# Loads in the order of first use at the start and between the two FFN stages, and a longer allowance for weight loads, in a Macaron transformer block

## The chip, the core and the metric

The kernel runs on one core of a Trainium2 chip. The core has TensorE (PE, matrix products), VectorE (DVE), ScalarE (ACT) and GpSimd (POOL), which run side by side and wait for each other by semaphores. SyncE (SP) issues the transfers between the chip's memory and the on-chip buffers. Each engine runs its own instructions strictly in the order in which the program holds them, so an instruction that waits holds up all that stand behind it on its engine. The metric is the device time of one execution in microseconds (us).

## The reference, cut to what matters

One block for 1024 tokens of width 1024, in fp32: a feed-forward network (FFN), a mix of two attentions, and a second FFN.

```python
def swiglu(h, w_in, w_out):                       # w_in 1024 x 5632, w_out 2816 x 1024
    gate, up = jnp.split(h @ w_in, 2, axis=-1)
    return (jax.nn.silu(gate) * up) @ w_out

x = x + 0.5 * swiglu(rms_norm(x, ffn1_norm), ffn1_w_in, ffn1_w_out)
h = rms_norm(x, mix_norm)
proj = h @ w_mix_in                               # q, k, v of both attentions, gates
...                                               # A: window of 128 tokens, with sinks
...                                               # B: compressed keys (compress_kv), selected
...                                               #    blocks and a window of 512, gated
x = x + mix @ w_mix_out
x = x + 0.5 * swiglu(rms_norm(x, ffn2_norm), ffn2_w_in, ffn2_w_out)
```

## The kernel before

**Products.** The 1024 tokens are 8 tiles of 128 (`x_74` to `x_81` are their on-chip buffers; in between they are reused as scratch, which is why they turn up in other roles). A product in fp32 accuracy is made of three fast products (`mm3`, L249 to L251): every operand is split into a high part (`...h`) and a low part (`...l`), and PE adds high·high, low·high and high·low. So each block of weights is loaded raw (`wraw`, 128x512, a ring of four buffers), its high part `whi` is made on ACT (L454) or POOL (L456), and its low part `wlo` on DVE (L459), which needs both.

**Input stage** (`first_stage`, L576). The 2816 hidden columns are 22 blocks of 128. The first two blocks are computed plainly, in pieces as the token tiles arrive: DVE scales a tile by its norm (L519), PE transposes it ("flips", `ntr`, L311), ACT and DVE split it (`xn0h`, `xn0l`), and PE multiplies. The other 20 blocks use a scheme of seven products in place of eight, which needs sums and differences of operands: differences of raw weights on DVE (L729), and additions of the partial results on DVE (L795), which also free the PSUM buffers `lg`, `pv` and `mo` for the next product. Side jobs (`sums_of`, L706) form the sums of w_out and of the activations that the output stage needs and store them in memory (`as_0A`, `as_10S`, ...).

**Output stage** (`second_stage`, L861). It loads those sums of activations back as `graw` (ring of five), splits them into `gph` (ACT, L454) and `gpl` (DVE, L459), and multiplies them with blocks of w_out. Both FFNs use these two functions.

**Between the FFNs.** The projection is followed by normed queries `qsp` (DVE, L1070), which PE transposes (`qtr`, L1077), ACT copies (`qst`, L1083) and SP stores (`qd`). Beside it, DVE prepares `cpw` (L1369, L1371) from the weights `cw` of the compressed keys.

**The order of the work** is not written out by hand. `Plan` (L110) takes tasks with an engine, a cost, a position, dependences, the ring buffers that they need, and a `tail`: the time after the task's end until its result may be used. It repeatedly places the task that can start first by these figures, and the one with the lower position where several can start within 0.08 us. The order in which tasks are placed is the order of the instructions on each engine. The figures change nothing else: what an instruction waits for on the chip is its real data. A weight load (`fetch`, L436) has `tail=2.2`.

The functions that the change touches:

Of the kernel before, what the change touches and what calls it, by code (L numbers as in the profile page):

```python
# [19 lines left out]
NT = 8  # L20
D = 1024
KD = 8
FF = 2816
# [14 lines left out]
CPOS, CAT = 1.0, 9  # L38
MM = 0.2275


# [15 lines left out]
class Units:  # L57
# [7 lines left out]
    def add(self, width, parts):  # L65
        self.units.append((width, parts))
        return len(self.units) - 1
# [120 lines left out]
def block_kernel(  # L188
# [246 lines left out]

    def fetch(src, pos, deps=(), k=4):  # L436

        b, us = {}, []

        def emit():  # L440
            b["r"] = ws.place()
            dma(b["r"].rearrange("p (k f) -> p k f", k=k) if k > 1 else b["r"], src)
        fetched.append(add("S", 0.75, pos, emit, deps=deps, after=fetched[-1:], takes=[(r_raw, us)], tail=2.2))
        return b, fetched[-1], us
# [122 lines left out]
    XS = [dr.tile([128, D], F32, name=f"xs{t}") for t in range(NT)]  # L567

    def open_in(p):

        t = {k: [p.tile([128, 4, 512], F32R, name=k + s) for s in "hl"] for k in ("S4", "A22", "S2", "S1", "S3")}
        t["A21"] = t["S4"]
        t["A11"], t["A12"] = XN0
        return t

    def first_stage(layer, w_in, w_out, opn, scaled, units_, side, pos, weigh, at0, pieces, opened, xa=()):  # L576

        ready = {}

        def src(n, j, part):  # L580
            return dram_ap(w_in, 512 * j * 2 * FF + part * FF + n * 128, [[4 * 2 * FF, 128], [2 * FF, 4], [1, 128]])

# [33 lines left out]
        for n in range(PLAIN):  # L616
            for j in range(2):
                for part in range(2):
                    b, t, us = fetch(src(n, j, part), pos - 8.0 + 4 * n, deps=at0)
                    W[n, j, part] = split(b, t, us, pos - 4.0 + 8 * n, weigh)  # L620
# [77 lines left out]
        def sums_of(k, at, srcs, deps, names, where, ops):  # L698

            us, ld = [[] for _ in range(4)], []  # L700
            for j in range(4):
                ld.append(add("S", 0.75, at, lambda j=j: dma(side_in()[j], srcs[j]()), deps=deps, takes=[(side_at[j], us[j])],
                              tail=2.2))
# [36 lines left out]
        for n in range(PLAIN, NF):  # L740
# [3 lines left out]
            for name, j, part in (("B11", 0, 0), ("B21", 1, 0), ("B12", 0, 1), ("B22", 1, 1)):  # L744
                raw[name] = fetch(src(n, j, part), at - 14.0)
            O = {}
# [108 lines left out]
    def second_stage(layer, w_out, at, opened, first_free, stored, p_out, X_ready, each, last=3):  # L855
# [7 lines left out]
        for m, (an, bn, bk, i, c) in enumerate(PRODUCTS):  # L863
# [7 lines left out]
            for k in range(NK):  # L871
                p0 = at + k * step
                b, ru = {}, []

                def load(k=k, an=an, b=b):
                    b["r"] = ring(p_out(), "graw", [128, 512], F32, 5)
                    dma(b["r"], AS[layer][k][an])
                first_ = [first_free] if m == 0 and k < 8 else []
                loads_g.append(add("S", 0.75, p0 - 9.0, load, deps=[stored[k, an]] + first_, after=[opened, loads_g[-1]],
                                   takes=[(r_g, ru)], tail=2.2))  # L880
                A = split(b, loads_g[-1], ru, p0 - 5.0, "A", pair, r_gp, g_chain)
                if bn[0] == "T":
# [4 lines left out]
                b, t, us = fetch(src, p0 - 9.0, dep, 1)  # L887
                ops.append((A, split(b, t, us, p0 - 5.0, "A")))
# [51 lines left out]
    r_y = Ring("hr", [128, 4, 8], F32, 6)  # L940
    new_plan([])
    load_x(0, n=2)
    load_gain(gain1, ffn1_norm)
    come = lambda at: add(None, 0.0, 0.0, lambda: None, tail=at)
    xt = [[come(3.3), come(4.05)]]
    for t in range(1, NT):
        n = 2 if t < 4 else 1
        xt.append([add("S", 1.46, 0.5 * t if t < 4 else 6.0 + t, lambda t=t, n=n: load_x(t, n=n),
                       deps=[come(2.0)], tail=2.2)])
    w_ = add(None, 0.0, 0.0, lambda: None, tail=1.4)  # L950
# [3 lines left out]
    for t in range(NT):  # L954
# [5 lines left out]
                                         lambda: [gain1[:, h] for h in HALF], 2.0, "G", [],   # L960
                                              [(0, 256), (256, 512)], none)

    def to_out():
        nonlocal p_nw, xn, p_o
        f_in.close()
        xn = xn_tiles(pool("p_xn", ph1))
        p_o = pool("p_out", f_out)
        p_nw = pool("p_nw", nws, side="right")
        mem["gain"] = p_nw.tile([128, D], F32, name="gainm")
        load_gain(mem["gain"], mix_norm)  # L970
        for key, qn_, kn_ in (("a", q_norm_a, k_norm_a), ("b", q_norm_b, k_norm_b)):
            gq[key] = cst.tile([128, HD], F32, name="gq" + key)
            gk[key] = p_o.tile([128, HD], F32, name="gk" + key)
            dma(gq[key], dram_ap(qn_, 0, [[0, 128], [1, HD]]))
            dma(gk[key], dram_ap(kn_, 0, [[0, 128], [1, HD]]))
    xn = p_o = None
    gq, gk = {}, {}
    f_out = ExitStack()
    opened = add("S", 2.0, at - 5.0, to_out, after=chain_[-1:])
    r_nx = Slots(2)  # L980
# [7 lines left out]
    at_out = at  # L988
    at = second_stage(0, ffn1_w_out, at, opened, chain_[4], stored_, lambda: p_o, again, each)
    for j, u in enumerate(CH3):  # L990
        conv(u, at - 6.0 + 0.5 * j)
    came = add(None, 0.0, at_out, lambda: None, deps=[opened], tail=20.0)
    bias_rows(at_out + 20.0, 1.5, [came])
# [341 lines left out]
    st_c = {}  # L1335
    c_open = add("S", 1.8, at - 12.0, cm_open, after=[p4_open], tail=2.2)

# [6 lines left out]
    for s in range(2):  # L1344
# [3 lines left out]
        for kh in range(2):  # L1348
            n, wb, wu = 2 * s + kh, {}, []

            def load_w1(n=n, wb=wb):
                wb["w"] = ring(mem["p4"], "cw1", [128, 8, 128], F32, 3)
                dma(wb["w"], dram_ap(cmp_w1, n * 1024 * 128, [[128, 128], [128 * 128, 8], [1, 128]]))
            ld = add("S", 0.5, at_c - 15.0, load_w1, after=[c_open], takes=[(r_w1, wu)], tail=4.0)
            for k0 in range(0, 8, 4):
# [623 lines left out]
    def each2(t, c, x_, pos):  # L1979
        add("S", 0.75, pos, lambda: dma(xout[t][:, HALF[c]], X[t][:, HALF[c]]), deps=[x_], tail=2.2)  # L1980
    second_stage(1, ffn2_w_out, at, opened2, chain_[4], stored_, lambda: p_o, again, each2)
    plan.run()
# [30 lines left out]
```

## Time and profile before

| | us |
|---|---|
| median of 3 runs | 1959.62 (1958.31 to 1960.3) |
| the profiled execution | 1957.43 |
| its span, first to last instruction | 1955.7 |
| PE busy | 1895.3 (97%) |
| DVE busy | 1358.0 (69%) |
| ACT busy | 917.2 (47%) |
| POOL busy | 405.2 (21%) |
| mean granted PE clock | 0.993 of full speed |

The profiled execution is 2.19 us under the median, and 1.73 us of it lie outside the span. The 97% is an average: PE has about 60 us of idle time in the whole span, and some stretches have more of it than others. The input stage of the first FFN runs from about 27 to 472 us, its output stage follows, the projection ends near 800, and the second FFN takes the time from about 1300 on, its output stage from 1740.

### The profile page before, as it was taken

The page shows a single profiled execution, that of the slowest core. Times are in us where ns is not written, and L with a number is a line of the kernel's source. Part 1 is how long each engine was busy: PE and PEld are TensorE (multiplying, and loading weights), DVE is VectorE, ACT ScalarE, POOL GpSimd, SP SyncE. Part 2 cuts the span into 40 slices and gives each one's busy share as a digit, 9 for nine tenths or more (in the row PEclk, how much of TensorE's full clock was granted, in tenths as well). Part 3 has the DMA queues.
Part 4 walks back from the last instruction along what each step waited for, and adds up shares of the span by engine and source line. Part 5 has one row for each costly group of instructions (what it writes and reads, how often), then busy time and mean ns, then how long its engine had stood idle before and what let it go on. Part 6 is the DMA issues. An engine that isn't in the chain of part 4 may idle for free.

```text
span 1955.7 us, 28018 instructions
## 1 busy us (share of the span) xinstructions
PE 1895.3 (97%) x9142; PEld 1580.6 (81%) x9142; DVE 1358.0 (69%) x3114; ACT 917.2 (47%) x1947; POOL 405.2 (21%) x544
## 2 busy tenths in 40 slices
PE   7999999999999999999899999989999999999999
PEld 5887888887888888887688778878878888878887
DVE  6687776565655667666888888875878666655553
ACT  4333333334444433345877888843333333344442
POOL 2111111111000011112754665521111111110000
PEclk9999999999999999999999999999999999999999
DMA  5277753235985436335201221021778432368662
GB/s 162 70 243 244 253 170 98 92 111 188 323 262 189 130 90 168 104 109 173 62 22 56 93 81 44 22 87 58 244 253 264 149 104 86 123 207 307 202 216 97
DMA packets 243955, 291.29 MB, mean 149 GB/s; under 512 B 24912, under 2 KB 138976, under 8 KB 243808
## 3 DMA queue, kind: packets, MB, share of 16 engines
q1 hardware_dynamic: 243808, 289.50, 46.1%
q8 instruction: 72, 1.18, 0.3%
q14 instruction: 75, 0.61, 0.1%
HBM read 202.24 MB, written 90.33 MB: 150 GB/s over the span
## 4 chain that ended last, share of the span: by engine, by line
PE 82%; DVE 7%; DMA 5%; ACT 2%; issue 2%; SPq 1%; POOL 1%; DVEq 0%; ACTq 0%; POOLq 0%
PE lg L249 11%; PE lg L251 11%; PE lg L250 11%; PE mo L249 5%; PE mo L251 5%; PE mo L250 5%; PE pv L249 3%; PE pv L251 3%; PE pv L250 3%; PE ptr L1815 3%; PE a L251 3%; PE a L249 3%; PE a L250 3%; PE pvo L1835 2%; PE lg L1640 2%
## 5 line engine op out<-in xcount | busy, mean ns | idle before, releaser
L459 DVE TENSOR_TENSOR wlo<-wraw,whi 128x512 fp32r<-128x512 f32 x290 | 220.1, 764 | 88.3 <-ACT whi L454 76.7
L799 POOL TENSOR_TENSOR x<-x,x 128x512 f32<-128x512 f32 x80 | 117.7, 1473 | 717.0 <-DVE x L795 675.7
L454 ACT ACTIVATE whi<-wraw 128x512 fp32r<-128x512 f32 x274 | 170.7, 623 | 126.8 <-PE lg L250 41.5
L459 DVE TENSOR_TENSOR gpl<-graw,gph 128x512 fp32r<-128x512 f32 x154 | 106.9, 697 | 131.5 <-ACT gph L454 131.1
L454 ACT ACTIVATE gph<-graw 128x512 fp32r<-128x512 f32 x154 | 96.8, 631 | 174.9 <-PE pv L250 82.0
L1825 DVE TENSOR_TENSOR pl<-ptr,ph 128x512 fp32r<-128x512 f32 x178 | 116.5, 685 | 16.1 <-ACT ph L1823 14.6
L791 ACT ACTIVATE x<-lg 128x512 f32<-128x512 f32 x96 | 57.4, 598 | 145.9 <-PE lg L251 145.9
L1823 ACT ACTIVATE ph<-ptr 128x512 fp32r<-128x512 f32 x178 | 98.8, 595 | 32.8 <-PE ptr L1815 31.5
L249 PE MATMUL a<-whi,gph 128*128 128x512 f32 x264 | 104.2, 395 | 5.7 <-ACT gph L454 5.7
L251 PE MATMUL a<-whi,gpl 128*128 128x512 f32 x264 | 103.6, 392 | 0.7 <-DVE gpl L459 0.7
L250 PE MATMUL a<-wlo,gph 128*128 128x512 f32 x264 | 103.5, 392 | 0.0
L87 POOL TENSOR_SCALAR whi<-wraw 128x512 fp32r<-128x512 f32 (+1 forms) x52 | 33.8, 653 | 331.2 <-PE mo L251 221.3
L249 PE MATMUL lg<-xn0h,whi 128*128 128x512 f32 (+1 forms) x264 | 100.4, 380 | 0.0
L250 PE MATMUL lg<-xn0l,whi 128*128 128x512 f32 (+1 forms) x264 | 99.8, 378 | 0.2 <-DVE xn0l L319 0.2
L251 PE MATMUL lg<-xn0h,wlo 128*128 128x512 f32 (+1 forms) x264 | 99.7, 378 | 0.0
L454 ACT ACTIVATE whi<-x 128x512 fp32r<-128x512 f32 x104 | 64.9, 628 | 73.2 <-PE lg L250 35.9
L459 DVE TENSOR_TENSOR wlo<-x,whi 128x512 fp32r<-128x512 f32 x104 | 71.4, 686 | 22.8 <-ACT whi L454 22.8
L795 DVE TENSOR_TENSOR x<-lg,x 128x512 f32<-128x512 f32 x72 | 49.6, 689 | 45.2 <-PE lg L251 45.1
L249 PE MATMUL lg<-whi,gph 128*128 128x512 f32 x198 | 77.0, 389 | 0.0
L250 PE MATMUL lg<-wlo,gph 128*128 128x512 f32 x198 | 77.0, 389 | 0.0
L251 PE MATMUL lg<-whi,gpl 128*128 128x512 f32 x198 | 77.0, 389 | 0.0
L249 PEld LDWEIGHTS a<-whi,gph 128*128 128x128 f32 x264 | 50.2, 190 | 16.6 <-ACT gph L454 6.5
(481 smaller groups left out, 5668.0 us busy)
## 6 DMA issues: line engine op xcount, KB each, us to landing
wraw<-in_ffn_w_in_dram SPq DMA_DIRECT2D x176, 256.0 KB, 3.5
wraw<-in_ffn_w_out_dram SPq DMA_DIRECT2D x66, 256.0 KB, 3.0
x<-in_ffn_w_out_dram SPq DMA_DIRECT2D x44, 256.0 KB, 4.6
qd<-qst SPq DMA_DIRECT2D x32, 256.0 KB, 2.2
xn0l<-qd SPq DMA_DIRECT2D x32, 256.0 KB, 2.8
wraw<-in_w_mix_in_dram SPq DMA_DIRECT2D x28, 256.0 KB, 2.8
x<-in_x_dram SPq DMA_DIRECT2D x12, 512.0 KB, 8.4
gain<-in_ffn_w_out_dram SPq DMA_DIRECT2D x22, 256.0 KB, 4.2
```

Source lines behind the costliest of these rows:

```text
L249: PE.matmul(o, ah, bh, start=first, stop=False, **kw)
L250: PE.matmul(o, ah, bl, start=False, stop=False, **kw)
L251: PE.matmul(o, al, bh, start=False, stop=last, **kw)
L454: ACT.activation(w["h"], b["r"], AF.Copy)
L459: low = add("D", 0.69, pos + 0.5, lambda: DVE.tensor_tensor(w["l"], b["r"], w["h"].bitcast(F32), op=OP.subtract), deps=chain[-1:])
L791: ACT.activation(b["r"], o["o"], act)
L795: return add("D", 0.69, at, lambda b=tb[k], o=bx[o]: DVE.tensor_tensor(b["r"], o["o"], b["r"], op=OP.add), deps=deps)
L799: return add("G", 1.25, at, lambda a=tb[a], b=tb[b]: POOL.tensor_tensor(a["r"], a["r"], b["r"], op=OP.mult), deps=deps)
L1640: PE.matmul(o, s.Q[:, h], ks[:, c0 + c:c0 + c + m], start=True, stop=False, skip_group_check=True)
L1815: PE.transpose(p[:, h * 128:(h + 1) * 128], s.P[h][:, c:c + 128], ident)
L1823: ACT.activation(st["ph"], st["p"], AF.Copy)
L1825: lo = add("D", 0.6, pos + 0.2, lambda st=st: DVE.tensor_tensor(st["pl"], st["p"], st["ph"].bitcast(F32), op=OP.subtract), deps=[hi])
```

## The change

The instructions of the program stay the same in kind and number; their order changes, by five edits.

1. At the start, the loads of the token tiles and of the first eight weight blocks are put in one chain on SP (`raws1`), so that they alternate.
2. `LATE = 4.5` takes the place of 2.2 as the tail of the loads of w_in from block 2 on, of w_out and its sums in the output stage, of the side jobs, and of `graw` (3.0 for the first two).
3. At the change of stages `to_out` only opens the buffers. The loads of the norm gains (`gainm`, `gqa`, `gka`, `gqb`, `gkb`) become a task of their own, `parameters`, placed later. The first eight `graw` loads wait for an earlier product of the input stage (`chain_[2]` in place of `chain_[4]`) in both FFNs; only the split into `gph` waits for the later one.
4. The opening of the compressed keys' buffers (`c_open`) is planned at 2.3 in place of 1.8.
5. A load of `cw` costs 1.5 in the plan and not 0.5, has a tail of 2.5 in place of 4.0, and depends on one of the projection's half tiles.

```diff
+LATE = 4.5
...
-    def fetch(src, pos, deps=(), k=4):
+    def fetch(src, pos, deps=(), k=4, tail=2.2):
...
-                    b, t, us = fetch(src(n, j, part), pos - 8.0 + 4 * n, deps=at0)
+                    b, t, us = raws[n, j, part] if raws else fetch(src(n, j, part), pos - 8.0 + 4 * n, deps=at0)
...
-                raw[name] = fetch(src(n, j, part), at - 14.0)
+                raw[name] = fetch(src(n, j, part), at - 14.0, tail=LATE)
...
-                first_ = [first_free] if m == 0 and k < 8 else []
-                loads_g.append(add("S", 0.75, p0 - 9.0, load, deps=[stored[k, an]] + first_, after=[opened, loads_g[-1]],
-                                   takes=[(r_g, ru)], tail=2.2))
-                A = split(b, loads_g[-1], ru, p0 - 5.0, "A", pair, r_gp, g_chain)
+                first_ = first_free if m == 0 and k < 8 else [none, none]
+                loads_g.append(add("S", 0.75, p0 - 9.0, load, deps=[stored[k, an], first_[0]], after=[opened, loads_g[-1]],
+                                   takes=[(r_g, ru)], tail=3.0 if m == 0 and k < 2 else LATE))
+                A = split(b, add(None, 0.0, p0, lambda: None, deps=[loads_g[-1], first_[1]]), ru, p0 - 5.0, "A", pair,
+                          r_gp, g_chain)
...
-    load_gain(gain1, ffn1_norm)
     come = lambda at: add(None, 0.0, 0.0, lambda: None, tail=at)
-    xt = [[come(3.3), come(4.05)]]
-    for t in range(1, NT):
-        n = 2 if t < 4 else 1
-        xt.append([add("S", 1.46, 0.5 * t if t < 4 else 6.0 + t, lambda t=t, n=n: load_x(t, n=n),
-                       deps=[come(2.0)], tail=2.2)])
+    xt, raws1 = [[come(3.3), come(4.05)]] + [None] * 7, {}
+    fetched[-1] = come(0.75)
+    fetched.append(add("S", 1.46, -20.0, lambda: load_gain(gain1, ffn1_norm), after=fetched[-1:], tail=2.2))
+    for w_ in (1, (0, 0, 0), (0, 0, 1), 2, (0, 1, 0), (0, 1, 1), 3, (1, 0, 0), (1, 0, 1), 4, (1, 1, 0), (1, 1, 1), 5, 6, 7):
+        if type(w_) is tuple:
+            raws1[w_] = fetch(in_src(ffn1_w_in, *w_), -20.0)
+        else:
+            fetched.append(add("S", 1.46, -20.0, lambda t=w_: load_x(t, n=2 if t < 4 else 1), after=fetched[-1:], tail=2.2))
+            xt[w_] = [fetched[-1]]
...
-    opened = add("S", 2.0, at - 5.0, to_out, after=chain_[-1:])
+    opened = add(None, 0.0, at - 5.0, to_out, after=chain_[-1:])
+    asked = add("S", 2.4, at + 14.0, parameters, deps=[add(None, 0.0, at, lambda: None, after=[opened], deps=chain_[-1:], tail=8.0)])
...
-    at = second_stage(0, ffn1_w_out, at, opened, chain_[4], stored_, lambda: p_o, again, each)
+    at = second_stage(0, ffn1_w_out, at, opened, (chain_[2], chain_[4]), stored_, lambda: p_o, again, each)
...
-    c_open = add("S", 1.8, at - 12.0, cm_open, after=[p4_open], tail=2.2)
+    c_open = add("S", 2.3, at - 12.0, cm_open, after=[p4_open], tail=2.2)
...
-            ld = add("S", 0.5, at_c - 15.0, load_w1, after=[c_open], takes=[(r_w1, wu)], tail=4.0)
+            ld = add("S", 1.5, at_c - 15.0, load_w1, deps=half1[4 + n:5 + n], after=[c_open], takes=[(r_w1, wu)], tail=2.5)
```

Line numbers after the change are higher by 1 from L40, by 2 from the input stage's loops on, and by 10 from the output stage's opening on.

**The start on SP.** Before, in the order of issue:

```order
L256 DMA x_74<-in_x_dram 128x512 x2
L256 DMA gain_398<-in_ffn_norm_dram 128x1024
L256 DMA wraw<-in_ffn_w_in_dram 128x4x128 x4
L256 DMA x_75<-in_x_dram 128x512 x2
L256 DMA x_76<-in_x_dram 128x512 x2
L256 DMA wraw<-in_ffn_w_in_dram 128x4x128 x4
L256 DMA x_77<-in_x_dram 128x512 x2
```

The same place on SP after the change:

```order
L257 DMA x_74<-in_x_dram 128x512 x2
L257 DMA gain_398<-in_ffn_norm_dram 128x1024
L257 DMA x_75<-in_x_dram 128x512 x2
L257 DMA wraw<-in_ffn_w_in_dram 128x4x128 x2
L257 DMA x_76<-in_x_dram 128x512 x2
L257 DMA wraw<-in_ffn_w_in_dram 128x4x128 x2
L257 DMA x_77<-in_x_dram 128x512 x2
L257 DMA wraw<-in_ffn_w_in_dram 128x4x128 x2
```

The second tile `x_75` moved from behind four weight blocks to directly behind the gain, and the weight blocks come in pairs between the tiles.

**The start on DVE** after the change, behind the making of `ident` (the rows of one element per partition are the norm of a tile, rows of several kinds in a fixed sequence):

```order
L503 TENSOR_SCALAR hr<-hr 128x1
L520 SCALAR_TENSOR_TENSOR x_74<-x_74,hr,gain_398 128x1024
L460 TENSOR_TENSOR wlo<-wraw,whi 128x512 x2
L509 TENSOR_SCALAR hr<-hr 128x1
L503 TENSOR_SCALAR hr<-hr 128x1
L473 RECIPROCAL hr<-hr 128x1
L474 SCALAR_TENSOR_TENSOR hr<-hr 128x1
L475 TENSOR_TENSOR hr<-hr 128x1
L476 SCALAR_TENSOR_TENSOR hr<-hr 128x1
L460 TENSOR_TENSOR wlo<-wraw,whi 128x512 x2
L520 SCALAR_TENSOR_TENSOR x_75<-x_75,hr,gain_398 128x1024
```

Before, four `wlo` stood ahead of all norms and the two scalings L519 of `x_74` and `x_75` followed each other; now the first tile's scaling stands ahead of all `wlo`, and the second's behind all four.

**The change of stages on SP.** Before, behind the last six `wraw` of the input stage:

```order
L256 DMA gainm<-in_mix_norm_dram 128x1024
L256 DMA gqa<-in_q_norm_a_dram 128x64
L256 DMA gka<-in_k_norm_a_dram 128x64
L256 DMA gqb<-in_q_norm_b_dram 128x64
L256 DMA gkb<-in_k_norm_b_dram 128x64
L256 DMA graw<-as_0A_110 128x512
L256 DMA graw<-as_1A_118 128x512
L256 DMA as_10A_191<-x_81 128x512
```

After the change, behind the same six `wraw`:

```order
L257 DMA graw<-as_0A_110 128x512
L257 DMA graw<-as_1A_118 128x512
L257 DMA graw<-as_2A_126 128x512
L257 DMA graw<-as_3A_134 128x512
L257 DMA as_10A_191<-x_81 128x512
L257 DMA graw<-as_4A_142 128x512
```

Five loads of parameters stood ahead of the first `graw`; four `graw` now come first, and the five stand 15 transfers further on.

**Compressed keys on DVE.** Before, around the fourth and fifth `qsp`:

```order
L1045 TENSOR_SCALAR hr<-hr 128x4
L1369 TENSOR_SCALAR cpw_7075<-cw_7115,cpos 128x128
L1371 SCALAR_TENSOR_TENSOR cpw_7075<-cw_7115,cpos,cpw_7075 128x128 x3
L1070 TENSOR_TENSOR qsp<-qn,qsp 128x4x64
L472 RECIPROCAL hr<-hr 128x4
```

After, from the fourth `qsp` (the first row) to the fifth (the last):

```order
L1080 TENSOR_TENSOR qsp<-qn,qsp 128x4x64
L1177 COPY gates<-lg 128x3x2x4
L473 RECIPROCAL hr<-hr 128x4
L474 SCALAR_TENSOR_TENSOR hr<-hr 128x4
L475 TENSOR_TENSOR hr<-hr 128x4
L476 SCALAR_TENSOR_TENSOR hr<-hr 128x4
L1054 TENSOR_REDUCE hr<-sq 128x4
L1055 TENSOR_SCALAR hr<-hr 128x4
L1071 TENSOR_TENSOR qn<-lg,hr 128x256
L1379 TENSOR_SCALAR cpw_7075<-cw_7167,cpos 128x128
L1381 SCALAR_TENSOR_TENSOR cpw_7075<-cw_7167,cpos,cpw_7075 128x128 x3
L1080 TENSOR_TENSOR qsp<-qn,qsp 128x4x64
```

The four `cpw` instructions moved from ahead of the fourth `qsp` to ahead of the fifth. On SP the first two `cw` loads moved from ahead of the first `qd` store to behind the second.

## Rows read from the trace of the kernel before

**Rows 1.** The profile page, busy time of each engine.
```profile
PE 1895.3 (97%) x9142; PEld 1580.6 (81%) x9142; DVE 1358.0 (69%) x3114; ACT 917.2 (47%) x1947; POOL 405.2 (21%) x544
```

**Rows 2.** Waits of PE, whole span: total us, times, longest.
```profile
PE ntr L311 <- DVE x L519: 9.8, 2, 9.5
...
PE a L249 <- ACT gph L454: 5.7, 2, 4.4
...
PE pv L249 <- DVE x L795: 3.6, 2, 2.5
...
PE qtr L1077 <- DVE qsp L1070: 3.0, 1, 3.0
...
PE lg L249 <- DVE x L795: 1.4, 1, 1.4
...
PE mo L249 <- DVE x L795: 1.2, 1, 1.2
```

**Rows 3.** Timeline of PE at the start: start, us; [idle before].
```profile
18.50 3.69 PE L311 MATMUL ntr<-ident,x 128*128 128x128 f32 x16 [9.50 <-DVE x L519]
...
26.68 0.56 PE L249 MATMUL lg<-xn0h,whi 128*128 128x256 f32 x1
```

**Rows 4.** DMA issues 0 to 3 us: count, KB each, us to landing.
```profile
x<-in_x_dram SPq DMA_DIRECT2D x2, 256.0 KB, 2.9
gain<-in_ffn_norm_dram SPq DMA_DIRECT2D x1, 512.0 KB, 6.1
wraw<-in_ffn_w_in_dram SPq DMA_DIRECT2D x2, 256.0 KB, 6.6
```

**Rows 5.** Two windows: length, busy of each engine, PEclk, DMA share, GB/s.
```profile
2.00:25.00 23.00, 10.42 (x40) 6.81 (x39) 12.62 (x29) 9.40 (x28) 6.03 (x8) 1.00 0.98 305
20.00:60.00 40.00, 36.39 (x232) 33.10 (x231) 35.69 (x75) 23.00 (x54) 11.54 (x8) 0.96 0.24 84
```

**Rows 6.** Timeline of DVE at the start.
```profile
10.58 2.73 DVE L459 TENSOR_TENSOR wlo<-wraw,whi 128x512 fp32r<-128x512 f32 x3 [0.51 <-POOL whi L456]
...
16.86 3.13 DVE L519 SCALAR_TENSOR_TENSOR x<-x,hr,gain 128x1024 f32<-128x1024 f32 x2
```

**Rows 7.** Timeline of PE, the first matmul behind four stalls.
```profile
161.90 0.79 PE L249 MATMUL pv<-A22h,whi 128*128 128x512 f32 x1 [2.50 <-DVE x L795]
...
477.01 0.80 PE L249 MATMUL a<-whi,gph 128*128 128x512 f32 x1 [4.40 <-ACT gph L454]
...
771.84 0.51 PE L1077 MATMUL qtr<-identr,qsp 128*128 128x128 f32 x4 [2.96 <-DVE qsp L1070]
...
1741.15 0.50 PE L249 MATMUL a<-whi,gph 128*128 128x512 f32 x1 [1.27 <-ACT gph L454]
```

**Rows 8.** Windows behind the first three of them, columns as in 5.
```profile
162.00:166.00 4.00, 4.00 (x11) 3.17 (x12) 2.53 (x5) 0.00 (x0) 1.27 (x1) 0.61 0.81 241
477.00:484.00 7.00, 6.99 (x19) 5.53 (x20) 5.42 (x9) 3.98 (x7) 0.00 (x0) 0.60 0.99 336
772.00:776.00 4.00, 4.00 (x22) 4.00 (x22) 2.75 (x12) 2.24 (x7) 0.34 (x1) 0.59 0.27 97
```

**Rows 9.** Timeline of SP's queue at the change of stages.
```profile
468.90 0.42 SPq L256 DMA_DIRECT2D gainm<-in_mix_norm_dram  x1
...
471.26 0.43 SPq L256 DMA_DIRECT2D graw<-as_0A  x1
```

**Rows 10.** Timeline of ACT at the change of stages.
```profile
473.19 0.62 ACT L454 ACTIVATE whi<-wraw 128x512 fp32r<-128x512 f32 x1
476.32 1.29 ACT L454 ACTIVATE gph<-graw 128x512 fp32r<-128x512 f32 x2 [2.51 <-DMA graw<-as_0A]
```

**Rows 11.** Timeline of DVE, two waits for loads.
```profile
155.91 0.69 DVE L729 TENSOR_TENSOR x<-wraw 128x512 f32<-128x512 f32 x1 [4.21 <-DMA wraw<-in_ffn_w_in_dram]
...
769.91 0.29 DVE L1369 TENSOR_SCALAR cpw<-cw,cpos 128x128 f32<-128x128 f32 x1 [3.42 <-DMA cw<-in_cmp_w_dram]
```

**Rows 12.** Timeline of SP's queue, the first loads of cw.
```profile
763.59 1.06 SPq L256 DMA_DIRECT2D cw<-in_cmp_w_dram  x2
```

More of the change, by code (lines that the diff above doesn't have):

```diff
@@ L442, in emit @@
             dma(b["r"].rearrange("p (k f) -> p k f", k=k) if k > 1 else b["r"], src)
-        fetched.append(add("S", 0.75, pos, emit, deps=deps, after=fetched[-1:], takes=[(r_raw, us)], tail=2.2))
+        fetched.append(add("S", 0.75, pos, emit, deps=deps, after=fetched[-1:], takes=[(r_raw, us)], tail=tail))
         return b, fetched[-1], us
@@ L567, in block_kernel, with in_src @@
     XS = [dr.tile([128, D], F32, name=f"xs{t}") for t in range(NT)]
+    def in_src(w_in, n, j, part):
+        return dram_ap(w_in, 512 * j * 2 * FF + part * FF + n * 128, [[4 * 2 * FF, 128], [2 * FF, 4], [1, 128]])
     def open_in(p):
@@ L574, in open_in, with first_stage @@
         return t
-    def first_stage(layer, w_in, w_out, opn, scaled, units_, side, pos, weigh, at0, pieces, opened, xa=()):
+    def first_stage(layer, w_in, w_out, opn, scaled, units_, side, pos, weigh, at0, pieces, opened, xa=(), raws=None):
         ready = {}
-        def src(n, j, part):
-            return dram_ap(w_in, 512 * j * 2 * FF + part * FF + n * 128, [[4 * 2 * FF, 128], [2 * FF, 4], [1, 128]])
+        src = lambda n, j, part: in_src(w_in, n, j, part)
         def flip(name, q, t, c, at, deps, free=()):
@@ L702, in sums_of @@
                 ld.append(add("S", 0.75, at, lambda j=j: dma(side_in()[j], srcs[j]()), deps=deps, takes=[(side_at[j], us[j])],
-                              tail=2.2))
+                              tail=LATE))
             prev = ld
@@ L886, in second_stage @@
                                        [[D, 128], [1, 512]]), []
-                b, t, us = fetch(src, p0 - 9.0, dep, 1)
+                b, t, us = fetch(src, p0 - 9.0, dep, 1, LATE)
                 ops.append((A, split(b, t, us, p0 - 5.0, "A")))
@@ L960, in block_kernel @@
                                          lambda: [gain1[:, h] for h in HALF], 2.0, "G", [],
-                                              [(0, 256), (256, 512)], none)
+                                              [(0, 256), (256, 512)], none, raws=raws1)
     def to_out():
@@ L969, in to_out, with parameters @@
         mem["gain"] = p_nw.tile([128, D], F32, name="gainm")
+    def parameters():
         load_gain(mem["gain"], mix_norm)
@@ L988, in block_kernel @@
     at_out = at
-    at = second_stage(0, ffn1_w_out, at, opened, chain_[4], stored_, lambda: p_o, again, each)
+    at = second_stage(0, ffn1_w_out, at, opened, (chain_[2], chain_[4]), stored_, lambda: p_o, again, each)
     for j, u in enumerate(CH3):
         conv(u, at - 6.0 + 0.5 * j)
-    came = add(None, 0.0, at_out, lambda: None, deps=[opened], tail=20.0)
+    came = add(None, 0.0, at_out, lambda: None, deps=[asked], tail=20.0)
     bias_rows(at_out + 20.0, 1.5, [came])
@@ L1980, in each2 @@
         add("S", 0.75, pos, lambda: dma(xout[t][:, HALF[c]], X[t][:, HALF[c]]), deps=[x_], tail=2.2)
-    second_stage(1, ffn2_w_out, at, opened2, chain_[4], stored_, lambda: p_o, again, each2)
+    second_stage(1, ffn2_w_out, at, opened2, (chain_[2], chain_[4]), stored_, lambda: p_o, again, each2)
     plan.run()
```

## The prediction

> **What bounds the kernel now.** I read the page's busy times first: PE works 1895.3 us [rows 1], so the kernel is bound by PE, and nothing that moves loads can win more than PE's idle time (some 60 us) and what its clock loses behind idle stretches. The second view is therefore the waits of PE [rows 2]. Only six lines of it touch what the change moves: the flips at the start wait 9.5 us in one piece for DVE's scaling, the first product of the output stage 4.4 us for `gph`, two products of the input stages 2.5 and 1.1 us (the 3.6 of `pv`) and two more 1.4 and 1.2 us for DVE's L795, and a flip of queries 3.0 us for `qsp`. Most of the rest lies in the attentions, whose order hardly changes. The third view is the timeline around each of these places [rows 3, 6, 7, 9 to 12], which says what the releasing engine itself waited for: in every case a load. The fourth is the granted clock behind the stalls [rows 8]: after idle times of 2.50, 4.40 and 2.96 us PE runs at 0.61, 0.60 and 0.59 over the next 4, 7 and 4 us, that is largely at 1.2 and not at 2.4 GHz. So such a stall costs its idle time and then (1 - 0.61) x 4 = 1.6, (1 - 0.60) x 7 = 2.8 and (1 - 0.59) x 4 = 1.6 us more. After the 1.27 us at 1741.15 the first matmul took 0.50 us where it took 0.80 behind the longer stalls [rows 7]: that one did not cost any clock.
>
> **The start.** In the first 25 us the transfers are the limit: the DMA share is 0.98 at 305 GB/s [rows 5]. The transfers land in about the order of issue (2.9 us after issue for the first tile, 6.1 for the gain, 6.6 for the first weight blocks [rows 4]), so I give each place in the queue the time that its bytes have now: 256 KB at 305 GB/s are 0.86 us. The gain, issued at about 1.6, lands near 7.7 as before. The first weight blocks, issued from 2.1 on, land near 8.7 and 9.5 before; their places now hold the two halves of `x_75`. Then the weights 1 and 2 land near 10.4 and 11.2, `x_76` near 12.1 and 12.9, weights 3 and 4 near 13.8 and 14.7. On DVE the first scaling takes 3.13 / 2 = 1.57 us [rows 6] and starts when the square of `x_75`, whose instruction stands ahead, is there: about 10, so it ends near 11.6, where both scalings ended at 20.0 before. Two `wlo` (2.73 / 3, so up to 0.91 each [rows 6]) and the norm of `x_75` follow until 14; then two `wlo` wait for weights 3 and 4 and for POOL's split of them (about 0.7 us, an estimate from ACT's 0.62 for the same split [rows 10]), and end near 16.2. The second scaling ends at 17.8, where the pair ended at 20.0. Behind it stand one pair of `xn0l` and the norm of `x_76` (2.5 us together), its scaling (near 21.5) and eight flips, 8 x 3.69 / 16 = 1.85 us [rows 3]: the first product starts near 22.9, against 26.68 [rows 3]. I take 4.0 us off. The bounds: 7, if the `wlo` come as the bytes allow and `x_75` is not held up; and 1 us of loss, if the fourth weight block is late, since `x_75` now stands behind it on DVE. What hides the gain is DVE: it is busy 35.69 of 40 us between 20 and 60 [rows 5]. But the same DVE work is done by the first product in both orders, only earlier, so I expect it to be kept. The last tile's loads end by 25 us in both, and it is not needed in the first product.
>
> **The change of stages in FFN 1.** SP issues five loads of parameters from 468.90 on and the first `graw` at 471.26 [rows 9], 2.4 us later. ACT waits 2.51 us for it and splits it at 476.32 [rows 10]. In the new order `graw` takes the place of `gainm` or an earlier one, so it lands near 474 or before and ACT goes on from its `whi`, which ends at 473.19 + 0.62 = 473.81 (that one stands behind the last product's copy and can't come earlier). `gph` then ends at 473.81 + 1.29 / 2 = 474.5 instead of 477.0: 2.5 us off, less 0.1 for `gpl`. PE's idle time is then 4.40 - 2.5 = 1.9 us, between the 1.27 that cost no clock and the 2.50 that did [rows 7, 8]. I take the side of the nearer one, 1.27 (0.6 apart each, so hardly more than even; the second FFN's change of stages runs through the same step without a fall), and 2.7 us of the clock's 2.8 come back. Sum 5.1, bounds 2.4 and 5.3. The parameters are issued some 15 transfers later; their readers come at the end of the output stage, more than 100 us on, so their move costs nothing. In FFN 2 the wait is 1.27 [rows 7], already at the floor that `whi` sets: nothing.
>
> **The input stages.** At 161.90 PE waits 2.50 us for L795 [rows 7]. DVE was late because a difference L729 waited 4.21 us for a weight block [rows 11] with all else queued behind it. The plan believed that block to be there 2.2 us after its issue; with 4.5 the order puts work that is ready ahead of L729, and the loads of the block ahead of those of the side job. I take the whole 2.5 + 1.6 = 4.1 off (bounds 0 and 4.1). Of the waits of 1.2, 1.4 and 1.1 us of the same kind [rows 2] I take 2.2 of 3.7, six tenths, since the order there changes in the same way but the loads' places on SP change less (bounds 0 and 3.7).
>
> **The compressed keys.** DVE waits 3.42 us for `cw` at 769.91 [rows 11] with the fourth `qsp` behind it, and PE 2.96 us for that `qsp` [rows 7], then 1.6 for the clock. Now the fourth `qsp` stands ahead: both go, 4.6 us. But a new wait comes: `cw` was issued at 763.59 [rows 12] and was there 6.3 us later; now it stands behind two stores of 256 KB, 2 x 0.86 us, so it lands near 771.6. Its four DVE instructions and the fifth `qsp` take 1.8 us, until 773.4, and PE wants the fifth at about 771.4: the fourth flip now stands six matmuls ahead of where PE waited (771.84 - 2.96 = 768.9), so at 768.2, and 24 matmuls of 280 columns follow, each 0.12 us (19 matmuls of 512 columns in 6.99 us at 0.60 [rows 8] make 0.22 at full clock, and 280/512 of that), beside the flip's own 0.3. So 1.9 to 2.0 of 4.6 come back as a new stall: 2.7 off, bounds 4.6 off and 1 lost (if the new stall grows past 3 us and costs its clock too).
>
> **New waits.** Nearly every second instruction of DVE's order in the two input stages changes its neighbour, and each L795 that comes later holds a PSUM buffer longer. No row shows what that costs. Below it is 0, since the waits that go are counted above; above two stalls like that at 161.90, 8 us. The nearest rows are the small ones (1.1 to 1.4 us [rows 2]): I take 2.0, about one and a half of them. `c_open`'s cost and PE's own few exchanges of neighbours I take at 0: PE's products are the same in number, and the moved flips have their operands.
>
> **Sum.** -4.0 - 5.1 - 4.1 - 2.2 - 2.7 + 2.0 = -16.1 us. The profiled execution of 1957.43 (span 1955.7, 1.7 outside) becomes 1941.3; it lies 2.2 under the median of 1959.62, which becomes 1943.5.
>
> **The rivals.**
> *The start is given back* (0.12). DVE, busy for 35.69 of 40 us from 20 to 60 [rows 5], is the bound of the plain blocks, and PE, begun earlier, waits for it later. Against it speaks that DVE is idle 10.4 of the 23 us from 2 to 25 [rows 5]. Without the 4.0: 1947.5.
> *The clock falls all the same* (0.11). 1.9 us of idle at the change of stages and the new stall at the fifth `qsp` each bring PE down to half speed: 2.7 and 1.6 us are lost, 1947.8.
> *The order of issue does not set the order of arrival* (0.06), so that the change of the start does not do what it says. Then `x_75` and the weights share the bandwidth, all land near 12, the start gains 0 and the sum gives 1947.5. Against it stand the three steps of 2.9, 6.1 and 6.6 us for issues within 2 us [rows 4]. The Trainium skill, "DMA: Bandwidth & Descriptors", section "Queues, rings and completion order", holds this rival up: each of the 16 DMA engines consumes its descriptors in ring order, but completion is "not FIFO per issuing engine". Were that strong enough to matter for whole transfers, the later, bigger gain would not have come ahead of the weights; the landing at 3.6, 7.7 and 8.7 us agrees with order kept, but shows three kinds of transfer only.
> *Slower* (0.07). An allowance of 4.5 us is longer than most loads need, so the plan puts splits and L729 behind additions although the data is there, and PE runs dry in the 40 Strassen-like blocks of the two input stages. One such stall of the size at 161.90 costs 4.1 us. The place would be PE's waits for `wlo` or L795 between 60 and 472 and between 1300 and 1740. With the 6.3 us of the input stages lost and no other new wait, 11.8 are won elsewhere, and from the third stall on (12.3) the kernel is slower; with five it is at 1959.6 - 11.8 + 20.5 = 1968.3. Against it: in the whole input stages PE waits only four times now [rows 2].
>
> **The numbers.** The forecast has 0.64, with its own range of 1936 to 1951 (a gain of 8.5 to 23.5: all the bounds that favour it give 4.1 + 3.7 + 7 + 5.3 + 4.6 = 24.7; half the terms at their poor end give about 8). About 0.2% of the time, 3.9 us, can be told from no change, so faster means under 1955.7. The first three rivals are all faster in themselves and could come together (4.0 + 4.3 less: 1951.8). The range 1935.5 to 1955 leaves out most of the slower case and the rarest gains. Faster: 0.64 + 0.29 less 0.06 for cases that add up badly, 0.87; same 0.08; slower 0.05, most of the last rival.
>
> **What would show it.** The first product at 22 to 24 us; PE's wait for `gph` at the change of stages under 2 us, and the clock of the 4 us behind it near 1.00; no wait of 2.5 us near 160; the wait for `qsp` gone at the fourth and 1 to 2.5 us long at the fifth. Wrong would make it: a first product at 26 or later, half clock behind the change of stages, or PE waits for DVE's L795, `wlo` or L729 of more than 4 us in sum in the input stages.

## The result and the profile after

The changed kernel took 1940.72 us (median of 4 runs, 1940.07 to 1942.83) against 1959.96 for the kernel before beside it (4 runs, 1958.31 to 1963.69): 0.9901 of it, with a 95% interval of 0.9884 to 0.9918. Run once more in a later batch it took 1941.70 (1940.63 to 1943.15), ratio 0.9900 (0.9884 to 0.9915). The forecast was 1943.5, so the kernel gained 19.2 us where 16.1 was worked out. The profiled execution took 1940.19, which is 17.24 less than the profiled one of before; its span is 1938.4.

Where that went is read best from PE. It runs the same 9142 matmuls, with a few neighbours exchanged, so the start of the same matmul in the two timelines says how much was won up to there (all in us):

| matmul | before | after | won so far | won in between |
|---|---|---|---|---|
| first product `lg<-xn0h,whi` | 26.68 | 21.99 | 4.7 | 4.7 (start) |
| `pv<-A22h,whi` behind the first stall | 161.90 | 154.69 | 7.2 | 2.5 (idle) |
| eighth matmul behind it | 165.05 | 156.28 | 8.8 | 1.6 (clock) |
| `mo<-A22h,whi` | 203.01 | 192.77 | 10.2 | 1.5 |
| last product of the input stage | 472.21 | 461.83 | 10.4 | 0.1 |
| first of the output stage | 477.01 | 464.00 | 13.0 | 2.6 (idle) |
| 17 matmuls on, at full clock in both | 483.59 | 471.70 | 11.9 | -1.1 |
| first product behind the compressed keys' stalls | 777.25 | 762.45 | 14.8 | 2.9 |
| `lg<-A22h,whi`, second FFN | 1430.80 | 1414.55 | 16.3 | 1.4 |
| `pv<-A22h,whi`, second FFN | 1470.27 | 1452.63 | 17.6 | 1.4 |
| last product of the second input stage | 1739.50 | 1721.68 | 17.8 | 0.2 |
| end of the span | 1955.7 | 1938.4 | 17.2 | -0.6 |

**The start.** PE's timeline of after (start, us, [idle before and what ended it]), which answers to [rows 3]:

```profile
10.72 1.98 PE L312 MATMUL ntr<-ident,x 128*128 128x128 f32 x8 [1.73 <-DVE x L520]
17.09 1.98 PE L312 MATMUL ntr<-ident,x 128*128 128x128 f32 x8 [4.39 <-DVE x L520]
20.39 1.95 PE L312 MATMUL ntr<-ident,x 128*128 128x128 f32 x8 [1.31 <-issue]
21.99 0.56 PE L250 MATMUL lg<-xn0h,whi 128*128 128x256 f32 x1
```

The first flips come 7.8 us earlier, the second tile's flips wait 4.39 us for its scaling, and 4.7 us remain at the first product. DVE's first two scalings:

```profile
9.38 1.28 DVE L520 SCALAR_TENSOR_TENSOR x<-x,hr,gain 128x1024 f32<-128x1024 f32 x1
...
15.76 1.28 DVE L520 SCALAR_TENSOR_TENSOR x<-x,hr,gain 128x1024 f32<-128x1024 f32 x1
```

The DMA issues from 2.0 to 2.9 us (count, KB each, median us to landing) show that `x_75` took the place of the weights:

```profile
gain<-in_ffn_norm_dram SPq DMA_DIRECT2D x1, 512.0 KB, 6.0
x<-in_x_dram SPq DMA_DIRECT2D x2, 256.0 KB, 6.4
```

Issued at 2.1 and 2.6, its halves land near 8.5 and 9.0, where the first weights landed before [rows 4].

**The input stages.** PE's waits of after from 60 to 466 us hold no L797 (the L795 of before) at all; these two rows, which belong to the change of stages, are the whole answer:

```profile
PE a L250 <- ACT gph L455: 1.8, 1, 1.8
PE a L252 <- DVE gpl L460: 0.7, 1, 0.7
```

DVE's waits for weight blocks from 60 to 455 us were 18.1 us before (14.8 in seven for `x`, 3.3 in five for `ext`, all at L729) and are now this row alone (total, times, longest); from 1290 to 1715 they fell from 14.5 us (11.2 and 3.3) to 2.0 (1.1 and 0.9):

```profile
DVE x L731 <- DMA wraw<-in_ffn_w_in_dram: 2.2, 2, 1.3
```

**The change of stages.** PE in the first FFN and in the second, for [rows 7]:

```profile
464.00 0.50 PE L250 MATMUL a<-whi,gph 128*128 128x512 f32 x1 [1.78 <-ACT gph L455]
...
465.46 0.80 PE L252 MATMUL a<-whi,gpl 128*128 128x512 f32 x1 [0.65 <-DVE gpl L460]
...
1723.86 0.50 PE L250 MATMUL a<-whi,gph 128*128 128x512 f32 x1 [1.78 <-ACT gph L455]
...
1725.32 0.50 PE L252 MATMUL a<-whi,gpl 128*128 128x512 f32 x1 [0.73 <-DVE gpl L460]
```

ACT at the first of them no longer waits for the load, as it did in [rows 10]. It runs the copy of the last product, a `whi` and then `gph` back to back:

```profile
462.31 0.60 ACT L793 ACTIVATE x<-lg 128x512 f32<-128x512 f32 x1 [2.32 <-PE lg L252]
462.81 0.62 ACT L455 ACTIVATE whi<-wraw 128x512 fp32r<-128x512 f32 x1
463.32 2.18 ACT L455 ACTIVATE gph<-graw 128x512 fp32r<-128x512 f32 x4
```

And the windows behind both places (length, busy of the five engines, granted clock, DMA share, GB/s):

```profile
464.00:471.00 7.00, 6.35 (x15) 4.72 (x16) 4.50 (x7) 2.37 (x5) 0.60 (x2) 0.54 0.90 302
1724.00:1731.00 7.00, 6.27 (x27) 4.89 (x28) 5.18 (x9) 3.59 (x7) 0.11 (x1) 1.00 0.97 332
```

The same pair of waits is followed by half clock in the first FFN and by full clock in the second. The second FFN is also worse off than before: 1.78 + 0.73 us where it had 1.27 + 0.66. ACT there, before and after:

```profile
1739.98 0.60 ACT L791 ACTIVATE x<-lg 128x512 f32<-128x512 f32 x1 [2.33 <-PE lg L251]
1740.48 1.14 ACT L454 ACTIVATE gph<-graw 128x512 fp32r<-128x512 f32 x2
```

```profile
1722.17 0.60 ACT L793 ACTIVATE x<-lg 128x512 f32<-128x512 f32 x1 [2.32 <-PE lg L252]
1722.66 0.62 ACT L455 ACTIVATE whi<-wraw 128x512 fp32r<-128x512 f32 x1
1723.18 1.14 ACT L455 ACTIVATE gph<-graw 128x512 fp32r<-128x512 f32 x2
```

Before, `gph` stood directly behind the copy; now a `whi` stands between them, and PE's wait is 0.51 us longer.

**The compressed keys.** PE's first flip that waits there, and DVE ahead of it, for [rows 7] and [rows 11]:

```profile
761.25 0.52 PE L1087 MATMUL qtr<-identr,qsp 128*128 128x128 f32 x4 [1.62 <-DVE hr L473]
```

```profile
758.87 0.29 DVE L1379 TENSOR_SCALAR cpw<-cw,cpos 128x128 f32<-128x128 f32 x1 [1.41 <-DMA cw<-in_cmp_w_dram]
...
760.69 0.41 DVE L1080 TENSOR_TENSOR qsp<-qn,qsp 128x256 fp32r<-128x256 f32 x1
```

The stall has moved to the fifth flip and shrunk from 2.96 to 1.62 us, with full clock behind it (a window, columns as above):

```profile
761.00:765.00 4.00, 3.75 (x27) 3.60 (x28) 3.79 (x15) 1.61 (x4) 1.20 (x2) 1.00 0.51 148
```

### The profile page after: what moved, and what is told of

The parts are those of the page before. It is cut to its first block, busy times and chain, and to the rows that moved or that the text cites. A ratio compares the mean times of both kernels' runs of the same rounds, so it can differ in the third digit from the quotient of the medians.

```text
span 1938.4 us, 28044 instructions
## 1 busy us (share of the span) xinstructions
PE 1892.4 (98%) x9142; PEld 1580.0 (82%) x9142; DVE 1365.0 (70%) x3114; ACT 917.4 (47%) x1947; POOL 404.8 (21%) x544
## 4 chain that ended last, share of the span: by engine, by line
PE 92%; DVE 3%; ACT 2%; POOL 1%; DMA 1%; issue 1%; SPq 0%; DVEq 0%; ACTq 0%; POOLq 0%
PE lg L250 13%; PE lg L252 13%; PE lg L251 13%; PE mo L250 6%; PE mo L252 6%; PE mo L251 6%; PE pv L250 4%; PE pv L252 4%; PE pv L251 4%; PE ptr L1825 3%; PE a L252 3%; PE a L251 3%; PE a L250 3%; PE pvo L1845 2%; PE pvo L1844 2%; PE lg L1650 2%
## 5 line engine op out<-in xcount | busy, mean ns | idle before, releaser
L460 DVE TENSOR_TENSOR wlo<-wraw,whi 128x512 fp32r<-128x512 f32 x290 | 203.8, 708 | 74.9 <-ACT whi L455 70.8
L797 DVE TENSOR_TENSOR x<-lg,x 128x512 f32<-128x512 f32 x72 | 49.7, 690 | 53.1 <-PE lg L252 52.8
```

What stands on the lines that cost most here:

```text
L460: low = add("D", 0.69, pos + 0.5, lambda: DVE.tensor_tensor(w["l"], b["r"], w["h"].bitcast(F32), op=OP.subtract), deps=chain[-1:])
L797: return add("D", 0.69, at, lambda b=tb[k], o=bx[o]: DVE.tensor_tensor(b["r"], o["o"], b["r"], op=OP.add), deps=deps)
```

## The experiments

All are edits of the changed kernel, so their times are held against its 1940.7 and 1941.7; a ratio is to the kernel before on the same chip. Beside the first four kernels the one before took 1963.07 us (1957.96 to 1967.14), 3 us more than beside the changed kernel, so by the ratios their differences are smaller: 2.6 us for u_start, 6.1 for u_late, none for u_change, 2.2 for u_mid. What a part is worth is therefore read from the shift of PE's matmuls at its own place as well.

**One part undone at a time.** Each of four kernels puts one part back, word for word, and leaves the others.

*u_start* puts back the start (edit 1 of the diff).

> The changed kernel with the loads of the start back in their old order and chain. Theory (each part pays by itself, as the shifts of PE's matmuls between the two traces show): the first product goes back from 21.99 to about 26.7, the rest of the trace moves with it, so 4.5 to 4.7 us slower than the changed kernel's 1940.7, about 1945.3. Rival (DVE, busy 37 of 40 us behind it, gives the start back in part when it begins earlier): less than 3 us slower, with PE waits in 20 to 60 us gone that the changed kernel has.

1946.37 us (1945.12 to 1947.68), ratio 0.9914 (0.9891 to 0.9938): 4.7 to 5.7 us slower. PE:

```profile
18.32 2.83 PE L312 MATMUL ntr<-ident,x 128*128 128x128 f32 x12 [9.32 <-DVE x L520]
...
26.50 0.56 PE L250 MATMUL lg<-xn0h,whi 128*128 128x256 f32 x1
```

The first product is back at 26.50, 4.5 us later, and at the end of the input stage PE is 5.0 us late. The start pays by itself and is not given back.

*u_late* puts back the allowance:

```diff
-LATE = 4.5
+LATE = 2.2
...
-                                   takes=[(r_g, ru)], tail=3.0 if m == 0 and k < 2 else LATE))
+                                   takes=[(r_g, ru)], tail=LATE))
```

> The changed kernel with LATE back at 2.2 (and the first two graw loads too). Theory (the allowance alone removed the stalls of the input stages): the waits of 2.5, 1.2, 1.4 and 1.1 us for DVE's additions come back, with 1.6 us of half clock behind the first: 4.3 + 1.5 + 1.9 + 1.4 = 9.1 us slower, about 1949.8. Rival (the earlier start or the loads' new places shifted the collisions of loads away, and the allowance did little): under 4 us slower.

1949.95 us (1948.87 to 1950.68), ratio 0.9932 (0.9912 to 0.9951): 8.3 to 9.2 slower. PE's waits in the two input stages (60 to 460 and 1290 to 1725 us), the first two rows of each answer:

```profile
PE pv L250 <- DVE x L797: 2.2, 1, 2.2
PE mo L250 <- DVE x L797: 0.8, 1, 0.8
```

```profile
PE lg L250 <- DVE x L797: 3.1, 1, 3.1
PE pv L250 <- DVE x L797: 0.7, 1, 0.7
```

All four stalls are back with the other parts still in place, so it was the allowance that removed them. Against the first profile of the changed kernel PE loses 9.8 us in the two input stages and gets 3.3 and 0.6 us back at the changes of stages, where this kernel waits 1.27 + 0.66 us. Of its two long stalls only the one of 2.2 us is followed by half clock (0.57 from 158 to 162 us); behind the 3.05 us at 1422.68 the clock is 1.00 from 1421 to 1428.

*u_change* puts back edit 3 of the diff.

> The changed kernel with the parameters loaded ahead of the first graw again, and the first graw loads bound to the later product, in both FFNs. Theory: the first product of the first output stage waits 4.4 us again and not 1.8, with about the same half clock behind it: 2.0 us slower, about 1942.7; the second FFN's place unchanged. Rival (the new order behind the change of stages, with the parameters in the middle of the output stage, costs something that the old one did not): same or faster than 1940.7.

1942.22 us (1940.20 to 1945.79), ratio 0.9895 (0.9872 to 0.9918). The wait for `gph` is 4.00 us again and the one for `gpl` gone, 1.57 us more idle time than the changed kernel's 1.78 + 0.65. The clock behind it is 0.76 from 467 to 474 us, which costs 1.7 us; the first profile of the changed kernel lost 3.2 there. So PE loses 0.4 us at this place against that profile, and 1.8 against the control's below. The median is 0.5 to 1.5 us above the changed kernel's and the runs overlap. This part is worth little, and not told from nothing by the time.

*u_mid* puts back edits 4 and 5.

> The changed kernel with the opening of the compressed keys' buffers and the loads of cw as before. Theory: the stall of 3.0 us before the fourth flip of queries comes back with 1.4 to 1.6 us of half clock, and the stall of 1.6 us before the fifth goes: 2.7 us slower, about 1943.4. Rival (a stall of some length stays wherever cw's four instructions stand): within 1 us of 1940.7.

1945.94 us (1944.66 to 1947.64), ratio 0.9912 (0.9892 to 0.9933): 4.2 to 5.2 slower, more than the 2.7 expected. The old stall is back and longer than in the kernel before:

```profile
760.34 0.51 PE L1087 MATMUL qtr<-identr,qsp 128*128 128x128 f32 x4 [3.29 <-DVE qsp L1080]
...
766.35 0.51 PE L1087 MATMUL qtr<-identr,qsp 128*128 128x128 f32 x4 [0.82 <-DVE hr L473]
```

A second stall of 0.82 us has joined it. Level with the first profile of the changed kernel ahead of these flips, PE is 4.2 us late behind both. Its profiled execution took 6.95 us longer; most of the rest arises where the clock falls elsewhere (below).

**The control.** *after_again* is the changed kernel once more.

> The changed kernel itself once more, as a control for the granted clock. Theory (the same stalls lead to half clock or not by where they fall in time, so one program shows nearly the same falls each time): falls near 464, 904 and 1116 as before, time 1940 to 1943. Rival (they come by chance from run to run): falls at other places, such as 1277 or 1724, where kernels with one part undone show them.

The time is 1941.70. The falls of the clock are not at the same places. The windows at the two changes of stages of this run:

```profile
465.00:472.00 7.00, 6.13 (x20) 4.67 (x21) 4.91 (x8) 3.10 (x7) 0.74 (x2) 0.76 0.86 285
1724.00:1731.00 7.00, 5.77 (x18) 4.37 (x19) 5.00 (x7) 3.13 (x6) 0.76 (x1) 0.76 0.99 344
```

0.76 and 0.76 where the first profile had 0.54 and 1.00, behind the same waits of 1.78 and 0.65 to 0.73. The rival held: the fall behind this pair of waits comes and goes between executions. The other profiles here say the same. Nine of them, these two included, have this pair at 16 places; the clock over the 9 us behind it is 1.00 at four, 0.81 at nine and 0.62 at three of them, a loss of 0, 1.7 or 3.4 us and 1.6 on average. Behind 1.27 + 0.66 us it is 1.00 at all three places (before, second FFN; u_late, both). And of the 6.95 us of u_mid's profiled execution, 2.07 also lie between the two of one and the same kernel.

**What sets the rest at the change of stages.** *fill* keeps PE busy there:

```diff
+    w_ = chain_[-1]
+    for j in range(3):
+        w_ = add("P", 0.64, at - 6.0, lambda: warm_up(3), deps=[w_], takes=[(r_mo, [])])
     opened = add(None, 0.0, at - 5.0, to_out, after=chain_[-1:])
```

> The changed kernel with nine transposes of a constant on PE, whose result nobody reads, between the input and the output stage of the first FFN, where PE is idle for 1.78 us. Theory (it is the idle time of PE that brings the clock down there): the first product starts at the same time within 0.4 us, the clock behind it stays at full speed, about 2.5 us less the 0.4, so 2 us faster than 1940.7. Rival (the clock falls there for another reason, such as what PE does afterwards): no faster, or 0.3 us slower.

```profile
462.58 1.70 PE L488 MATMUL warm<-ident 128*128 128x128 f32 x9
464.53 0.50 PE L250 MATMUL a<-whi,gph 128*128 128x512 f32 x1 [0.25 <-ACT gph L455]
```

```profile
464.00:471.00 7.00, 6.02 (x27) 4.53 (x26) 6.24 (x10) 3.36 (x7) 1.13 (x2) 1.00 0.92 294
```

In this profile the clock stays at 1.00, but the time, 1940.60 (1938.41 to 1942.86), is not told from the changed kernel's. In the same profile the clock is 1.00 behind the second FFN's pair of waits too, which nothing fills. So this profile does not show that the filling did it: inconclusive.

*graw_soon* lets the plan believe the first two `graw` to be there sooner:

```diff
-                                   takes=[(r_g, ru)], tail=3.0 if m == 0 and k < 2 else LATE))
+                                   takes=[(r_g, ru)], tail=1.2 if m == 0 and k < 2 else LATE))
```

> The changed kernel with a tail of 1.2 in place of 3.0 for the first two graw loads, which moves ACT's first split gph ahead of the copy of the last product. Theory (at the change of stages the remaining idle of 1.78 + 0.65 us is set by ACT's order, where a split for the second step stands ahead of the first gph, and no longer by the load): the idle falls to about 0.4 us in both FFNs, and the half clock behind it in the first FFN (2.5 us) goes: 2.0 + 2.5 + 2.1 = 6.6 us faster than 1940.7, about 1934. Rival (the landing of graw still sets it, so that ACT only waits at another instruction): within 1.5 us of 1940.7.

1934.44 us (1933.79 to 1936.91), ratio 0.9865 (0.9847 to 0.9882): 6.3 to 7.3 us faster than the changed kernel. ACT and PE at the first change of stages, and the windows behind both:

```profile
462.59 0.63 ACT L455 ACTIVATE gph<-graw 128x512 fp32r<-128x512 f32 x1 [2.29 <-DMA graw<-as_0A]
463.12 0.58 ACT L793 ACTIVATE x<-lg 128x512 f32<-128x512 f32 x1
```

```profile
463.27 0.50 PE L250 MATMUL a<-whi,gph 128*128 128x512 f32 x1 [0.74 <-ACT gph L455]
```

```profile
463.00:470.00 7.00, 6.73 (x28) 5.29 (x29) 5.43 (x8) 4.58 (x10) 1.66 (x2) 1.00 0.92 286
1719.00:1726.00 7.00, 6.75 (x28) 5.28 (x29) 4.29 (x6) 4.64 (x10) 1.31 (x1) 1.00 0.92 314
```

Now ACT does wait for the load, PE waits 0.74 us and not 1.78 + 0.65, and the clock is full behind both places. At the two changes of stages PE wins 4.5 and 1.7 us against the first profile of the changed kernel, and 3.1 and 3.1 against the control's: 6.2 and 6.3 us, nearly all that the time shows. So what the changed kernel still lost there was ACT's order: a copy of the last product and a `whi` for the second step stood ahead of the first `gph`, because the plan with a tail of 3.0 believed the load to come later. u_late, whose tail was 2.2 there, had 1.27 + 0.66.

**The start once more.** *start_late* gives the first eight weight blocks `tail=LATE`, which puts the second scaling ahead of all `wlo`.

> The changed kernel with a tail of 4.5 in place of 2.2 for the first eight weight blocks, which puts the scaling of x_75 on DVE ahead of all wlo. Theory (the start is now bound by DVE's order, with the second scaling held back by splits of weights): the flips of x_75 start near 13 and not at 17.09, the first product near 20.8 and not at 21.99, 1.2 us faster. Rival (the landings of weights and tiles bound it): first product within 0.4 us of 21.99.

```profile
12.76 1.13 PE L312 MATMUL ntr<-ident,x 128*128 128x128 f32 x4 [0.60 <-DVE x L520]
...
20.86 0.56 PE L250 MATMUL lg<-xn0h,whi 128*128 128x256 f32 x1
```

The first product comes 1.1 us earlier, and the second tile's flips start at 12.76, as expected. But the first flips also start 0.54 us earlier than in the changed kernel's profile (10.18 and 10.72), with the same loads and DVE instructions ahead of them. From the first flips to the first product it takes 10.68 us here and 11.27 there (11.27 to 11.40 in all nine profiles with the changed kernel's start), so DVE's order is worth 0.6 us of the 1.1 and the landing of the loads in this execution the rest. The time, 1940.71 (1938.69 to 1940.92), is 0 to 1 us below the changed kernel's, too little to be told.

**The size of the allowance.** *late33* and *late70* change `LATE = 4.5` to 3.3 and 7.0.

> The changed kernel with LATE = 3.3, about the median landing time of the weight loads in the input stage (3.3 us). Theory (the allowance has to exceed the landing in the bursts, 5 to 6 us, and not the median): some of DVE's waits for weight blocks come back, 3 to 12 us of them in both input stages where 4.5 has none listed and 2.2 has 29, and PE waits of 1 to 3 us: 1 to 4 us slower than 1941. Rival (the median suffices): within 1 us of 1941.

1940.67 us (1938.14 to 1944.29): as fast. DVE's waits for weight blocks from 60 to 455 us are back:

```profile
DVE x L731 <- DMA wraw<-in_ffn_w_in_dram: 6.5, 4, 2.6
...
DVE ext L731 <- DMA wraw<-in_ffn_w_in_dram: 6.1, 3, 3.9
```

With 8.8 + 7.5 us in the second input stage that is 28.9 us, not much less than the 32.6 of the kernel before; but PE's waits for L797 in both stages are 0.3 us, where they were 6.2. PE takes 1.2 and 1.0 us more for the two stages than in the first profile of the changed kernel. The theory fell in its second half: DVE's waits as such cost little. That they cost where an addition that PE needs is queued behind, and that the order at 3.3 no longer has it so, is argued here from the totals and not traced wait by wait.

> The changed kernel with LATE = 7.0. Theory (once it covers the landing, more allowance costs nothing as PE's order is the same): within 1.5 us of 1941, which is what the clock's falls at other places can move. Rival (too long an allowance puts splits and differences behind work that could wait, the forecast's way to a slower kernel): PE waits for DVE or ACT of more than 3 us in the input stages and a time above 1944.

1943.95 us (1941.58 to 1946.31): 2.2 to 3.2 slower. The input stages show no wait of PE but 0.6 us, so the rival's place was wrong; a new one stands in the output stage, on PE and on ACT:

```profile
494.24 0.50 PE L250 MATMUL a<-whi,gph 128*128 128x512 f32 x1 [1.61 <-ACT gph L455]
```

```profile
493.56 2.66 ACT L455 ACTIVATE gph<-graw 128x512 fp32r<-128x512 f32 x4 [10.62 <-DMA graw<-as_9A]
```

The load that ACT waits for was issued late. SP in late70 and, below it, in the changed kernel:

```profile
477.81 5.82 SPq L257 DMA_DIRECT2D x<-in_x_dram  x8
483.87 0.33 SPq L257 DMA_DIRECT2D graw<-as_9A  x1
```

```profile
474.26 0.39 SPq L257 DMA_DIRECT2D graw<-as_9A  x1
...
476.41 5.66 SPq L257 DMA_DIRECT2D x<-in_x_dram  x8
```

Too long an allowance does cost: here it put a load that PE needs behind eight that could wait, and PE loses 2.2 us at this place against the first profile of the changed kernel.

**Both improvements.** *combo* joins graw_soon and start_late.

> The changed kernel with the tail of 1.2 for the first two graw loads and the tail of 4.5 for the first eight weight blocks together. Theory (the two places are apart and add up): first product near 20.8, idle of 0.7 us at both changes of stages without half clock behind; 6.3 us less for the one, 0.9 for the other, about 1933.8. Rival (the start's gain is lost behind it, as the time of that part alone, 1940.71, says): no faster than 1934.4.

1934.57 us (1933.85 to 1935.12), ratio 0.9869 (0.9854 to 0.9884): the same as graw_soon alone. Its first product starts at 21.85, 10.63 us behind its first flips: the order gains its 0.6 us again, but the first tile was scaled 1.0 us later than in start_late. The loads' landing differs by that much between runs. The fastest version stays graw_soon's, one number away from the changed kernel.

## Why the prediction was right, and where not

- **The start**: 4.0 forecast, 4.7 won in the profile, and kept, as u_start shows by undoing it. The chain was as worked out: first scaling, two `wlo`, norm, two `wlo`, second scaling, and so on. Its end came at 21.99 and not 22.9; a scaling took 1.28 us and not 1.57, half of the pair's 3.13. The eight other profiles with this start have the first product at 21.85 to 22.89, so 3.8 to 4.8 us are won and the 4.7 lies at the good end. That DVE would give it back did not happen, and the order of issue did set the order of arrival: ACT reads `x_75` from 8.42 us on and not from 12.09.
- **The first input stage's long stall**: 4.1 forecast, 4.1 won (2.5 + 1.6). u_late shows the cause. Of the three small ones 2.2 of 3.7 were forecast and 4.6 won: all of them went, and the slower first matmul behind each as well. This term was undersized.
- **The change of stages**: 5.1 forecast, 1.5 won (2.6 idle, less 1.1). This step failed, and its half clock was named beforehand as a sign of being wrong. The idle time fell to 1.78 us as worked out (1.9), but "I take the side of the nearer one" was a guess between 1.27 and 2.50, and in the profile half clock cost more than before (0.54 over 7 us against 0.60): the rival "The clock falls all the same" came true at one of its two places. The control shows that there was no side to take: behind 1.78 + 0.7 us the fall comes and goes, at 12 of 16 places. Nor was the second FFN's 1.27 us "the floor that `whi` sets": there only the copy stood ahead of `gph`. Missed besides: 0.1 us was allowed for `gpl`, it took 0.65. And the second FFN's place, put at nothing, lost 0.6 us: the longer tail of the first `graw` moved a `whi` ahead of `gph` there too, in the way of the rival "Slower", though once and not in the input stages.
- **The compressed keys**: 2.7 forecast, 2.9 won in the profile; the new stall was put at 1.9 to 2.0 us and took 1.62, with no half clock. Undone alone this part is worth 4.2 to 5.2, since a longer stall and a second one come back; so the price of such a stall depends on what has changed around it.
- **New waits**: 2.0 forecast, none found in the input stages of the changed kernel. This was the term that made the forecast too small, together with the small stalls.

The sum came out 3 us short in the medians, 1.1 short between the two profiled executions. What was too much (3.6 in the failed step, 0.6 in the second FFN) was more than covered by what was too little: 0.7 at the start, 2.4 in the small stalls, 0.2 at the keys and 2.0 for new waits. So that the total came this near is in part luck: errors of up to 3.6 us cancelled, and two profiled executions of one and the same kernel already differ by 2.07 us.

## What to carry to other kernels

A plan's allowance for a load is not a safety margin: both too short and too long put the wrong instruction first on an in-order engine, and one number for two early loads was worth 6 us here. Look at what is queued behind a waiting instruction, not at how long it waits: 33 us of DVE's waits for weights went with 6.2 idle us of PE in one order, 29 us with 0.3 in another. And where a profile shows a fall of the clock behind a stall of 1 to 3 us, run the same program again before that fall is put into a sum.

## What the runs showed of the hardware

- The granted clock behind the same two waits of 1.78 and 0.65 to 0.73 us was 1.00 over 7 us (after, second FFN), 0.76 (after_again, both) and 0.54 (after, first FFN). Behind 0.74 to 0.76 us it was 1.00 in both places of graw_soon. Behind 2.50 and 2.96 us it fell in the kernel before, behind 3.05 us in u_late it did not.
- A DVE split took 1.34 us and not the usual 0.69 where POOL was at work at the same moment. POOL and DVE at the change of stages of the changed kernel:

```profile
462.99 1.27 POOL L801 TENSOR_TENSOR x<-x,x 128x512 f32<-128x512 f32 x1 [1.02 <-ACT x L793]
```

```profile
463.46 1.34 DVE L460 TENSOR_TENSOR wlo<-wraw,whi 128x512 fp32r<-128x512 f32 x1 [2.63 <-ACT whi L455]
```

DVE began 0.80 us before POOL's end at 464.26 and needed 0.54 us more after it. The Trainium skill, "SBUF — State Buffer", section "SBUF: two separate sides", says that a DVE operation with two SBUF inputs and a GpSimd operation that reads SBUF exclude each other from a shared port pair, and "the other fully blocks". This pair of rows agrees in the main: DVE lost 0.65 us in an overlap of 0.80. The next instruction on DVE is the `gpl` that PE waited 0.65 us for.
